# A decoder layer's up-projection: three of its weight tiles formed early instead of two, and the input projection's tiles in a new order

## The chip, the cores and the metric

The kernel runs on one core of a Trainium2 chip. The metric is the device time of one execution in microseconds (us). Before the change the median of three runs is 1663.53 us (1659.94 to 1669.49).

The core has five engines with a queue of instructions each: TensorE (PE in the profile; its weight loads are PEld), VectorE (DVE), ScalarE (ACT), GpSimd (POOL) and SyncE (SP). An engine executes its queue in order, and an instruction that waits holds up those behind it. DMA transfers are issued from the queues of SP, ACT and POOL.

## The reference

One decoder layer for 1024 prompt tokens and 64 sample tokens (8 sequences of 8), 1088 in all, width 1024, in float32:

```python
h = rms_norm(x, norm1) * (1 + scale1) + shift1
z = h @ w_in            # queries, 6 key/value tiles, gates, conv, pooling
x = x + gate1 * (concat[attention, conv, pooling] @ w_out)
h = rms_norm(x, norm2) * (1 + scale2) + shift2
x = x + gate2 * ((silu(h @ w_a) * (h @ w_b)) @ w_down)     # hidden width 2816
```

The queries `q` and two of the key tiles (`ks` for selected blocks, `kw` for the window) are normalised per head after the projection. The raw keys and values `kc`, `vc` are compressed into block keys; this is also done for the sample sequences' paged cache. The pooling mixer takes trailing means over 2, 4, 8 and 16 positions of its two tiles `p0`, `p1`.

## The kernel before, in words

**Precision.** A float32 product is made of three products of "hi" and "lo" parts: ACT copies a tile into a reduced format (hi, line 175), and DVE subtracts hi from it (lo, line 171). Forming a pair of parts is called a split below.

**Stages.** (1) The front: loading x, the adaLN rounds, the first norm, and the values and gates per token. (2) `input_projection` (line 885): 16 weight tiles of 128 columns, each multiplied with the 1088 tokens in three chunks (384, 384, 320). Each tile's weights are loaded into one of two `w_raw` buffers, and split, one tile ahead. In the order of line 901 they are kc, vc, six conv tiles, p0, ks, p1, kw, q0 to q3. (3) Attention for prompt and samples. (4) The output projection and second norm. (5) The up-projection. (6) The down-projection.

**Who sets the order.** The program is emitted by Python generators that share a clock of estimated engine times (`self.t`). `run` (line 85) always continues the ready task with the lowest priority number; `hold` makes a task wait, on that clock, for a condition. So the order of each engine's queue is fixed when the program is built. The tile framework then moves instructions within it by a simulation of its own, and adds the waits that the data and the reuse of buffers need. `late_ada` (16 steps of gate weights) and the compression of three sample sequences run as such tasks beside the input projection. `head_norm` (line 752) is the normalisation of a q, ks or kw chunk: a square on ACT, a matmul with a matrix of means, a square root on ACT, and on DVE a reciprocal (line 765) and a multiplication (line 766). `pooling_steps` (line 815) puts a chain of DVE additions after the last chunk of p0 or p1, then a matmul with the pooling weights, whose result `py` (one buffer) ACT stores to `mix_d`. A `hold` on `pooled` stands after each of the two.

**The up-projection.** Its weights are 22 tiles `j`, each with 128 columns of both halves. Tokens are taken in four quarters of 272, two quarters making a pair `p`. For one tile and one pair the 2 by 2 block product is done with seven products in place of eight (`PRODUCTS`, line 33); each needs a combination of weight blocks, split into hi and lo, and the same for the token blocks. `up` (line 1668) makes one such pass: 7 products of 12 matmuls. `operands` (line 1613) forms the token side of a pair, four times seven combinations (`b_t`) and splits (`b_hi`, `b_lo`). The passes go (0,0), (1,0), (2,0), (2,1), (1,1), (0,1), and from tile 3 on both pairs of one tile; the second pair's operands are formed while the first pair's passes run. `unit_weights` (line 1645) prepares the weights of the next run of passes: for a tile below `AHEAD_W` it loads the 14 ready parts from DRAM (`w_d`, line 1654), for the others it combines (`w_s`) and splits (`w_hi`, `w_lo`) them from two loads of 512 KB (`w_raw`, line 1498):

```python
raw[n] = j if j < AHEAD_W else tuple(self.weight_load(wp, self.i["wup"][j, x]) for x in range(2))
```

**Formed ahead.** `up_weights_ahead` (line 967) forms the seven pairs of one tile and stores them to `w_d`: two loads (`p_raw`), five combinations on POOL, seven splits on ACT and DVE (`p_hl`, two buffers), seven stores of 512 KB on SP's queue. It is called for tile 0 from `first_ahead` (line 961), when the front is done, and for tile 1 beside the four query tiles, in a pool "pre" which takes memory that the pooling tiles had. `self.formed` counts the tiles done. After vc the projection holds until tile 0 is formed, and frees its pool for the conv tiles; after q3 it holds until tile 1 is.

After the projection, attention begins with `key_stacks` (line 1042): the splits `kh`, `kl` of ks, kw and the compressed keys, then the queries' `qh`, `ql`.

Of the kernel before, what the change touches and what calls it, by code (L numbers as in the profile page):

```python
# [32 lines left out]
STORED = {1: 0, 2: 1, 3: 2, 5: 3, 6: 4, 7: 5, 4: 6}  # L33
HID = 2816
NH = HID // P
AHEAD_W = 2
PAGES = 32
NPOOL = 320
NCMP = 255
# [23 lines left out]
class Kernel:  # L63
# [110 lines left out]
    def split(self, hi, lo, src, n, ready=0.0, eng="dve"):  # L174
        self.nc.scalar.activation(hi, src, AF.Copy)  # L175
        r = self.use("act", 0.09 + n * 0.00084, ready)
        return self.combine(lo, src, hi.bitcast(F32), OP.subtract, n, r, eng)
# [707 lines left out]
    def input_projection(self, h):  # L885
        nc = self.nc
        yield from self.hold(lambda: self.ada_loaded >= 8)
        zp_ = self.pool("zout", "left")
        zp = zp_.__enter__()
        self.vt = zp.tile([P, 9, 256], F32, name="vt_")  # L890
        self.gates = zp.tile([P, 9, 24], F32, name="gates")
        self.vcp = zp.tile([64, P], F32, name="vcp")
        self.spawn(0.6, self.first_ahead())
        with self.pool("tok", "left") as tp:
            yield from self.token_part(tp, h)
        yield from self.hold(lambda: self.ahead)
        hn_, hn, pp_ = self.ahead
        zq_ = self.pool("zq", "left")
        self.q = zq_.__enter__().tile([P, 4, T], F32, name="q")
        self.zout = (zq_, zp_)  # L900
        order = ["kc", "vc", "cg0", "ch0", "bg0", "cg1", "ch1", "bg1", "p0", "ks", "p1", "kw", "q0", "q1", "q2", "q3"]
        self.ada2 = self.pool("ada2", "left")
        self.ada_pool = self.ada2.__enter__()
        with self.pool("z", "left") as z:
            load, split, get = self.weights(z, [self.i["win"][ORDER.index(n)] for n in order], raw_bufs=2, bufs=2)

            def tiles(names, step):
                for nm in names:
                    w = get()
                    load()  # L910
                    for ch, (c0, n) in enumerate(CHUNKS):
                        yield max(w[2], max(self.h_at[ch]))
                        acc = self.project(w, h, ch, n)
                        step(nm, ch, acc, c0, n)
                        self.z_steps += 1
                        if ch == 0:
                            split()

            def kcv(nm, ch, acc, c0, n):
                self.evac(self.kcv[:, nm == "vc", c0:c0 + n], acc, n)  # L920

            def qk(nm, ch, acc, c0, n):
                if nm[0] == "q":
                    out, gain, done = self.q[:, int(nm[1]), c0:c0 + n], self.qgain[:, 0:1], None
                else:
                    j = int(nm == "kw")
                    out, gain = self.ksw[:, j, c0:c0 + n], self.kgain[:, 1 + j:2 + j]
                    done = lambda: nc.gpsimd.dma_start(self.o["kskwT"][:, j, c0:c0 + n], out)
                self.spawn(0, self.head_norm(hn, out, acc, n, gain, done=done))

            load()
            load()
            split()
            self.spawn(0.5, self.late_ada())
            yield from tiles(["kc", "vc"], kcv)
            yield from self.hold(lambda: self.formed == 1)
            pp_.__exit__(None, None, None)
            nc.gpsimd.dma_start(self.o["kcvcT"], self.kcv)
            z0 = self.z_steps
            self.spawn(lambda: 0.9 if self.octets <= PACE * (self.z_steps - z0) else 1.5, self.compress_more())  # L940
            with self.pool("conv") as cv:
                for j in range(2):
                    st = dict(zip(("cg", "ch", "bg"), self.conv_steps(cv, j)))
                    yield from tiles([n + str(j) for n in ("cg", "ch", "bg")],
                                     lambda nm, ch, acc, c0, n: st[nm[:2]](ch, acc))
            with self.pool("pooling") as pl:
                self.pooled = 0
                for j, names in ((0, ["ks"]), (1, ["kw"])):
                    step = self.pooling_steps(pl, j)
                    yield from tiles(["p" + str(j)], lambda nm, ch, acc, c0, n: step(ch, acc))  # L950
                    yield from tiles(names, qk)
                    yield from self.hold(lambda: self.pooled > j)
            with self.pool("pre") as pp:
                self.spawn(0.6, self.up_weights_ahead(pp, 1))
                yield from tiles(["q0", "q1", "q2", "q3"], qk)
                yield from self.hold(lambda: self.formed == 2)
            yield from self.hold(lambda: self.prompt_at and self.heads == 18 and 5 in self.ada_at)
            hn_.__exit__(None, None, None)
        self.ada2.__exit__(None, None, None)

    def first_ahead(self):
        yield from self.hold(lambda: self.front_done)
        hn_, pp_ = self.pool("hn"), self.pool("pre")
        self.ahead = hn_, hn_.__enter__(), pp_
        yield from self.up_weights_ahead(pp_.__enter__(), 0)

    def up_weights_ahead(self, pool, j):

# [794 lines left out]
    def ffn(self, wp, fp, H, state, ahead):  # L1763
# [10 lines left out]
        def load(n):  # L1774
            if n < len(runs):
                j = runs[n][0]
                raw[n] = j if j < AHEAD_W else tuple(self.weight_load(wp, self.i["wup"][j, x]) for x in range(2))

# [365 lines left out]
    def build(self):  # L2144
# [32 lines left out]
        self.mix_d = self.dram.tile([P, 8, T], F32, name="mix_d")  # L2177
        self.w_d = self.dram.tile([AHEAD_W, P, 7, 2, 512], F32, name="w_d")
        self.formed = 0
# [155 lines left out]
```

## Time and profile before

| | |
|---|---|
| median of three runs | 1663.53 us |
| the profiled execution's own time | 1667.26 us |
| its span, first to last instruction | 1665.7 us |
| busy: PE, DVE, ACT, POOL | 1567.0, 1091.3, 778.7, 653.4 us |
| mean granted TensorE clock | 0.972 |
| forming of tile 0, first load to last store | 57.5 to 104 us |
| forming of tile 1, first load to last store | 311.6 to 344.5 us |
| first and last load of formed parts in the up-projection | 910.8 and 998.5 us |

In the profile's views, a row of a group names line, engine, operation, output and inputs, their shapes and how often it ran; behind the bar stand the group's busy time, the mean duration of one in ns, and the engine's idle time just before them with what ended it. A row of a view by stretches gives each engine's busy time (and number of instructions), the granted TensorE clock as a share of full speed, and the load of the DMA engines. A row of waits says which instruction waited for which, for how long in all, how often, and the longest. Rows of a timeline start with the time of the start and the duration in us.

### The profile page before, as it was taken

To read this page: it belongs to the slowest core of one execution; us is meant where nothing else is said; L and a number is where in the kernel's file an instruction comes from. 1 tells how busy PE (TensorE), PEld (TensorE's weight loads), DVE (VectorE), ACT (ScalarE), POOL (GpSimd) and SP (SyncE) were. 2 spreads that over 40 slices of the span, in tenths; PEclk is the share of its full clock that TensorE was granted. 3 is DMA by queue.
4 is the path that set the end of the run, shared out by engine and by line. 5 is a ranking of instruction groups with operands and counts; after the bars stand their busy time and mean duration, and the time that the engine had idled before them with its cause. 6 is when DMAs were issued, how large, how long until landed. Compare 5 with 4: busy or idle time off the path is not lost.

```text
span 1665.7 us, 35433 instructions
## 1 busy us (share of the span) xinstructions
PE 1567.0 (94%) x12569; PEld 1393.3 (84%) x12569; DVE 1091.3 (66%) x2646; ACT 778.7 (47%) x1828; POOL 653.4 (39%) x783
## 2 busy tenths in 40 slices
PE   6999999998999899899599989999999999899998
PEld 2899997886777566566399989999999999899998
DVE  4813224876465666766479878776777776477767
ACT  3522215335665567566466534443433443344444
POOL 3111010123343233222013266544555555688765
PEclk9999999997999899999799989999999999999999
DMA  9586664424567363244686554446433435976643
GB/s 334 186 281 179 184 202 155 149 77 149 159 179 220 99 197 101 64 132 134 199 307 196 199 201 173 145 145 212 151 139 139 143 139 197 380 258 245 218 162 125
DMA packets 195923, 302.12 MB, mean 181 GB/s; under 512 B 26353, under 2 KB 133170, under 8 KB 195426
## 3 DMA queue, kind: packets, MB, share of 16 engines
q1 hardware_dynamic: 175874, 272.20, 49.3%
q0 software_dynamic: 5856, 16.24, 3.1%
q10 hardware_dynamic: 14016, 11.41, 2.1%
q8 instruction: 100, 1.64, 0.4%
q14 instruction: 77, 0.63, 0.1%
HBM read 233.43 MB, written 70.53 MB: 182 GB/s over the span
## 4 chain that ended last, share of the span: by engine, by line
PE 75%; DVE 10%; ACT 6%; DMA 4%; issue 3%; POOL 1%; SPq 0%; ACTq 0%; DVEq 0%; POOLq 0%
PE bank L139 72%; PE bank L143 3%; DVE P L1123 2%; ACT P L1135 2%; DVE w_lo L171 1%; DMA w_raw<-in_wup 1%; DMA mixc<-mix_d 1%; DMA x<-x_d 1%; POOL P L1145 1%; DVE b_lo L171 1%; DMA stream<-in_cacheA 1%; ACT w_hi L175 1%; DMA w_raw<-in_wout 1%; DVE x L1889 0%; ACT L1135 0%
## 5 line engine op out<-in xcount | busy, mean ns | idle before, releaser
L139 PE MATMUL bank<-b_hi,w_hi 128*128 128x272 f32 x1232 | 352.3, 291 | 5.9 <-DVE f_g L1686 2.9
L139 PE MATMUL bank<-b_lo,w_hi 128*128 128x272 f32 x1232 | 355.3, 290 | 2.5 <-DVE b_lo L171 2.4
L139 PE MATMUL bank<-b_hi,w_lo 128*128 128x272 f32 x1232 | 350.3, 290 | 0.9 <-DVE w_lo L171 0.9
L139 PEld LDWEIGHTS bank<-b_hi,w_hi 128*128 128x128 f32 x1232 | 231.8, 190 | 9.0 <-ACT b_hi L175 3.8
L139 PEld LDWEIGHTS bank<-b_lo,w_hi 128*128 128x128 f32 x1232 | 234.1, 190 | 3.4 <-DVE b_lo L171 3.3
L139 PEld LDWEIGHTS bank<-b_hi,w_lo 128*128 128x128 f32 x1232 | 232.2, 190 | 1.1 <-DVE w_lo L171 1.1
L1145 POOL TENSOR_SCALAR P<-P,st 128x128 f32<-128x128 f32 (+10 forms) x192 | 109.0, 581 | 232.5 <-DVE st L1141 138.5
L171 DVE TENSOR_TENSOR w_lo<-w_raw,w_hi 128x512 fp32r<-128x512 f32 (+2 forms) x121 | 114.9, 959 | 79.7 <-ACT w_hi L175 79.2
L171 POOL TENSOR_TENSOR w_s<-w_raw 128x512 f32<-128x512 f32 (+1 forms) x88 | 125.2, 1422 | 70.6 <-DVE w_lo L171 52.7
L139 PEld LDWEIGHTS bank<-stream 128*128 128x128 f32 x1056 | 128.4, 200 | 15.7 <-issue 11.9
L175 ACT ACTIVATE w_hi<-w_raw 128x512 fp32r<-128x512 f32 (+2 forms) x122 | 81.1, 679 | 124.0 <-PE bank L139 83.8
L139 PE MATMUL bank<-stream 128*128 128x128 f32 x1056 | 134.6, 286 | 1.7 <-DMA stream<-in_cacheA 1.6
L1135 ACT ACTIVATE P<-P,st 128x128 f32<-128x128 f32 (+12 forms) x192 | 113.1, 590 | 46.1 <-DVE st L1129 29.4
L171 POOL TENSOR_TENSOR x<-x,d_m 128x272 f32<-128x272 f32 x136 | 117.0, 882 | 32.8 <-DVE x L1889 17.4
L139 PE MATMUL bank<-h_hi,w_hi 128*128 128x384 f32 (+1 forms) x384 | 129.3, 337 | 0.4 <-DVE q L766 0.4
L171 DVE TENSOR_TENSOR w_lo<-w_s,w_hi 128x512 fp32r<-128x512 f32 (+1 forms) x124 | 116.4, 940 | 17.2 <-ACT w_hi L175 14.9
L139 PE MATMUL bank<-h_hi,w_lo 128*128 128x384 f32 (+1 forms) x384 | 126.5, 329 | 0.0
L139 PE MATMUL bank<-g,w_hi 128*128 128x272 f32 x616 | 121.1, 292 | 5.7 <-DVE x L1889 5.7
L139 PE MATMUL bank<-h_lo,w_hi 128*128 128x384 f32 (+1 forms) x384 | 126.3, 329 | 0.0
L139 PE MATMUL bank<-g,d_hi 128*128 128x272 f32 x616 | 119.1, 289 | 1.4 <-DVE x L1892 1.2
L1889 DVE SCALAR_TENSOR_TENSOR x<-bank,mod,x 128x272 f32<-128x272 f32 (+1 forms) x200 | 90.1, 476 | 38.9 <-PE bank L139 25.5
L1716 POOL TENSOR_TENSOR f_g<-f_g,f_v 128x272 f32<-128x272 f32 x44 | 43.9, 998 | 152.9 <-DVE f_v L1686 131.7
(373 smaller groups left out, 3789.8 us busy)
## 6 DMA issues: line engine op xcount, KB each, us to landing
g<-g_d SPq DMA_DIRECT2D x63, 544.0 KB, 6.0
g_d<-f_s SPq DMA_DIRECT2D x57, 544.0 KB, 3.4
wada<-in_wada SPq DMA_DIRECT2D x96, 256.0 KB, 5.3
stream<-in_cacheA SPq DMA_DIRECT2D x192, 128.0 KB, 3.2
w_raw<-in_wup SPq DMA_DIRECT2D x40, 512.0 KB, 4.4
unit<-in_cacheB SPq DMA_DIRECT2D x152, 128.0 KB, 2.4
stream<-in_cacheB SPq DMA_DIRECT2D x104, 128.0 KB, 2.4
w_raw<-in_wout SPq DMA_DIRECT2D x24, 512.0 KB, 4.4
```

Of the source, the lines that this page charges most:

```text
L139: return self.nc.tensor.matmul(out, lhsT, rhs, start=start, stop=stop, skip_group_check=chain)
L143: return self.nc.tensor.transpose(out, in_, self.ident if ident is None else ident)
L171: (self.nc.vector if eng == "dve" else self.nc.gpsimd).tensor_tensor(out, a, b, op=op)
L175: self.nc.scalar.activation(hi, src, AF.Copy)
L1123: nc.vector.tensor_tensor_reduce(out=Pt[:, 2 * g + hl, col:col + n], in0=S[g][:, p0:p0 + n], in1=mk, scale=-1.0, scalar=3e38, op0=OP.add, ...
L1135: nc.scalar.activation(Ps, Ps, AF.Exp, scale=-1.0, bias=sy[:, g, 0:1], accum_out=sy[:, g, 1:2])
L1145: nc.gpsimd.tensor_scalar(Ps, Ps, sy[:, g, 3:4], 0.0, op0=OP.mult, op1=OP.add)
L1716: nc.gpsimd.tensor_tensor(g[:, 1], s1, v, op=OP.mult)
L1889: self.last_gate = nc.vector.scalar_tensor_tensor(out[:, :n], acc[:, :n], self.mod[:, 5, m, 0:1], out[:, :n], op0=OP.mult, op1=OP.add)
```

## The change

Tile 2 of the up-projection is formed in the input projection too. `first_ahead` forms tiles 0 and 1, one after the other; tile 2 takes the place of tile 1 beside the last query tiles, of which there are now two there. The order of the input projection becomes kc, vc, ks, kw, the conv tiles, p0, q0, p1, q1, q2, q3. The hold that frees the first "pre" pool stands after kw, and waits for two tiles. In the up-projection the run of tile 2 finds ready parts in `w_d`. `compress_more`, the compression of the prompt's keys, is started after kw in place of after vc.

```diff
-AHEAD_W = 2
+AHEAD_W = 3
...
-        order = ["kc", "vc", "cg0", "ch0", "bg0", "cg1", "ch1", "bg1", "p0", "ks", "p1", "kw", "q0", "q1", "q2", "q3"]
+        order = ["kc", "vc", "ks", "kw", "cg0", "ch0", "bg0", "cg1", "ch1", "bg1", "p0", "q0", "p1", "q1", "q2", "q3"]
...
             yield from tiles(["kc", "vc"], kcv)
-            yield from self.hold(lambda: self.formed == 1)
+            yield from tiles(["ks", "kw"], qk)
+            yield from self.hold(lambda: self.formed == 2)
             pp_.__exit__(None, None, None)
...
-                for j, names in ((0, ["ks"]), (1, ["kw"])):
+                for j, names in ((0, ["q0"]), (1, ["q1"])):
...
             with self.pool("pre") as pp:
-                self.spawn(0.6, self.up_weights_ahead(pp, 1))
-                yield from tiles(["q0", "q1", "q2", "q3"], qk)
-                yield from self.hold(lambda: self.formed == 2)
+                self.spawn(0.6, self.up_weights_ahead(pp, 2))
+                yield from tiles(["q2", "q3"], qk)
+                yield from self.hold(lambda: self.formed == 3)
...
-        yield from self.up_weights_ahead(pp_.__enter__(), 0)
+        pp = pp_.__enter__()
+        for j in range(2):
+            yield from self.up_weights_ahead(pp, j)
```

## The prediction

> **What bounds the kernel now.** I read the page's head first, then its chain of work that ended last, then the stretches of the two places the change touches, and there the waits and groups.
>
> ```profile
> span 1665.7 us, 35433 instructions
> PE 1567.0 (94%) x12569; PEld 1393.3 (84%) x12569; DVE 1091.3 (66%) x2646; ACT 778.7 (47%) x1828; POOL 653.4 (39%) x783
> ...
> PE 75%; DVE 10%; ACT 6%; DMA 4%; issue 3%; POOL 1%; SPq 0%; ACTq 0%; DVEq 0%; POOLq 0%
> ```
>
> TensorE sets the end for three quarters of the span. Time is to be won only where it waits or runs slowly. One such place is the start of the up-projection, where tile 2's weights are formed (columns: stretch, length, busy time and count of PE, PEld, DVE, ACT, POOL, granted clock, DMA):
>
> ```profile
> 946.00:956.00 10.00, 9.95 (x80) 9.73 (x78) 9.77 (x23) 7.54 (x16) 4.16 (x4) 1.00 0.06 20
> 956.00:967.00 11.00, 6.49 (x43) 5.63 (x43) 11.00 (x24) 4.05 (x11) 8.20 (x8) 0.95 0.49 157
> 967.00:973.00 6.00, 5.90 (x27) 5.93 (x28) 5.69 (x9) 2.33 (x6) 5.62 (x8) 0.52 0.30 111
> 973.00:980.00 7.00, 6.99 (x56) 6.77 (x55) 5.76 (x10) 2.57 (x7) 6.24 (x8) 1.00 0.23 82
> 980.00:984.00 4.00, 1.86 (x9) 1.42 (x10) 3.83 (x5) 1.51 (x5) 3.62 (x5) 0.87 0.12 29
> 984.00:990.00 6.00, 6.00 (x28) 5.87 (x28) 2.38 (x6) 1.35 (x4) 1.32 (x2) 0.52 0.98 348
> ```
>
> Undisturbed, PE does 8 matmuls per us (80 in 10 us, the first row). By that rate the next five rows should hold 88, 48, 56, 32 and 48; they hold 43, 27, 56, 9 and 28. What is missing is worth 5.6, 2.6, 0, 2.9 and 2.5 us: 13.6 us lost in 34. Half is waiting, and the rest a granted clock of 0.52 behind each wait. DVE is full in the same rows. The waits of PE from 935 to 1000, and DVE's and POOL's groups from 937 to 986:
>
> ```profile
> PE bank L139 <- DVE f_g L1686: 2.9, 1, 2.9
> PE bank L139 <- DVE b_lo L171: 2.4, 3, 0.8
> PE bank L139 <- DVE w_lo L171: 0.9, 1, 0.9
> PE bank L139 <- ACT b_hi L175: 0.5, 1, 0.5
> ```
> ```profile
> L171 DVE TENSOR_TENSOR b_lo<-b_t,b_hi 128x272 fp32r<-128x272 f32 x19 | 13.9, 761 | 0.2 <-ACT b_hi L175 0.2
> L171 DVE TENSOR_TENSOR w_lo<-w_s,w_hi 128x512 fp32r<-128x512 f32 x5 | 4.0, 794 | 0.0
> L171 DVE TENSOR_TENSOR w_lo<-w_raw,w_hi 128x512 fp32r<-128x512 f32 x2 | 1.4, 686 | 0.2 <-ACT w_hi L175 0.2
> L171 DVE TENSOR_TENSOR w_s<-w_raw 128x512 f32<-128x512 f32 x1 | 0.9, 907 | 0.0
> ...
> L171 POOL TENSOR_TENSOR b_t<-x1b 128x272 f32<-128x272 f32 x20 | 18.9, 961 | 18.3 <-ACT x1b L1603 13.9 <-DVE b_lo L171 2.6 <-issue 1.7
> ```
>
> Every wait of PE there is for DVE, or one step short of it. DVE does three things at once: it forms the second pair's operands (`b_lo`), empties PE's banks (`f_g`), and splits tile 2's weights (`w_lo`, seven in all).
>
> The other place is the end of the input projection:
>
> ```profile
> 104.00:132.00 28.00, 28.00 (x189) 25.82 (x188) 2.41 (x3) 3.60 (x7) 1.66 (x3) 1.00 0.72 228
> 283.00:311.00 28.00, 27.97 (x165) 22.93 (x164) 26.75 (x37) 11.58 (x24) 4.71 (x8) 1.00 0.53 154
> 311.00:339.00 28.00, 27.64 (x161) 26.28 (x160) 20.37 (x29) 10.55 (x21) 7.49 (x7) 1.00 0.45 164
> 339.00:366.00 27.00, 27.00 (x155) 25.68 (x154) 19.67 (x15) 7.30 (x14) 0.00 (x0) 1.00 0.17 59
> 366.00:378.00 12.00, 5.42 (x40) 4.61 (x38) 10.70 (x15) 4.55 (x9) 8.72 (x24) 0.89 0.39 115
> ```
>
> PE is full until 366, while the four query tiles take the third and fourth rows (55 us, 13.7 a tile). Early on DVE is nearly empty (2.41 of 28 us), and full when the pooling runs (26.75). Then comes the step to attention, where PE idles for DVE.
>
> **The change part by part.**
>
> *Tile 2 in the up-projection.* It removes two loads of `w_raw`, five combinations `w_s`, seven `w_hi` on ACT and seven `w_lo`. On DVE that is 4.0 + 1.4 + 0.9 = 6.3 us of the groups above. The work that PE waits for is a queue on DVE without gaps from 946 to 980, so what is taken out of it brings forward everything behind it: the banks emptied, the `x1b` that POOL's `b_t` wait for, and the last `b_lo`. PE gets its last late operand 6.3 us earlier. It doesn't win all 13.6: tile 2's pass then ends about 8 us earlier (5.6 + 2.6), and PE waits in one piece for the second pair's operands, which are late next. I take −6.3. The ends are 0, if POOL or the hand-offs between engines set the operands' pace, and −13.6, if the operands are never late.
>
> It adds 14 loads from `w_d` on SP's queue.
>
> ```profile
> L1654 SPq DMA_DIRECT2D w_hi<-w_d x28: 319/372/639, 910.8 to 998.0; - x28
> L1654 SPq DMA_DIRECT2D w_lo<-w_d x28: 319/383/656, 911.3 to 998.5; - x28
> ...
> DMA to landing us min/median/max: 2.6/4.6/8.7
> ```
>
> A pair of them costs SP some 0.8 us and lands in 4.6 us, 8.7 at worst. The buffers (nine of each) let a part be issued about seven products ahead, that is 84 matmuls or 10.5 us. SP holds only the stores of hidden tiles there, and DMA is at 0.06 in the row from 946. So I take 0, hidden behind the pass before; without that cover it would be 4.6 us once.
>
> *Tiles 0 and 1 in front.* Two loads, five combinations, seven splits and seven stores more run from about 104 to 137 us. DVE and POOL have the room (first row of the last table). On SP the stores wait for each split, and behind them stand the loads of the next weight tile, the gate weights and the cache; PE has a tile in hand. The ks and kw normalisations come to the same place, with their six stores on POOL's queue, behind which stand cache loads. I take 0. The bounds: 0, and +2 if one weight tile comes late once (below: six stores of one forming spread over 15.62 us on SP, less a tile of 13.7).
>
> *Tile 2 beside two query tiles.* Tile 1 was formed beside four:
>
> ```profile
> 320.54 1.29 POOL L171 TENSOR_TENSOR p_hl<-p_raw 128x512 f32<-128x512 f32 x1 [5.49 <-DMA mix_d<-py]
> ...
> 343.51 0.63 DVE L171 TENSOR_TENSOR p_hl<-p_hl 128x512 fp32r<-128x512 f32 x1
> ...
> 324.22 15.62 SPq L985 DMA_DIRECT2D w_d<-p_hl  x6
> ...
> POOL p_hl L171 <- DMA w_d<-p_hl: 12.0, 2, 6.8
> ```
> ```profile
> L765 DVE RECIPROCAL h_sq<-h_sq 128x384 f32<-128x384 f32 x7 | 17.9, 2551 | 13.5 <-ACT h_sq L762 13.5
> L171 DVE TENSOR_TENSOR p_hl<-p_hl 128x512 fp32r<-128x512 f32 x5 | 3.6, 724 | 0.0
> ```
> ```profile
> 366.72 1.05 ACT L175 ACTIVATE kh<-kv__93 128x1024 fp32r<-128x1024 f32 x1
> ...
> 377.83 0.89 PE L139 MATMUL bank<-kh,qh 64*128 64x192 f32 x2 [6.58 <-DVE q L766]
> ```
>
> It can't begin before the pooling's `py` has left the memory, and it took 23.6 us from 320.54 to 344.14, because the two `p_hl` buffers wait for their stores (12.0 us on POOL). The pooling now ends two tiles later, 27.5 us, so the forming ends near 371.6, while the last query product stays at 366. ACT's `kh` at 366.72 and DVE's `kl` then meet the last of the seven splits in their queues. Each split is 0.7 us on DVE and ACT; what must wait is the step to attention, where PE already waits 6.58 us. DVE's room holds the other splits: 19.67 of 27 us are busy from 339 on, without any forming after 344. I take +1.5, two splits; the bounds are 0 (all behind the keys) and +5 (the keys behind all).
>
> *The pooling holds.* After p1 PE has one tile (q1 in place of kw) until the pooling's product, as before. What PE did from 305 to 311.4 beside it:
>
> ```profile
> L139 PE MATMUL bank<-pe_x,pw 128*128 128x384 f32 (+2 forms) x8 | 2.3, 412 | 0.0
> L139 PE MATMUL bank<-wada,sc 128*32 128x512 f32 x8 | 2.1, 604 | 0.0
> ```
>
> The gate steps (`wada`), 2.1 us of fill, may be over by then; PE would idle as long, and do them earlier at no gain. I take 0, since the prompt's compression can fill it; the bounds are 0 and +2.1.
>
> **The sum**: −6.3 + 0 + 0 + 1.5 + 0 = −4.8 us on the profiled execution's 1667.3, which is 1662.5. That execution was 3.7 above the median of the runs, so on the median it is 1663.5 − 4.8 = **1658.7**. Attention's order is planned on clocks that the change shifts; no row prices that.
>
> The Trainium skill (TensorE: Matmul & The Clock Gate, What's actually happening) says that PE falls to half clock after an idle window of some 3.4 us. The trace has 0.52 after a wait of 2.9 us, and again after waits of at most 0.8 us close together, so the trace counts: a single wait of the kind left over by the change still costs a slow stretch. By the rule alone the second stretch, 2.5 us, would not be there before, nor in the 13.6.
>
> **The rivals.**
>
> *All of it is won (0.23).* With the splits gone DVE and POOL finish the second pair in time, as the planner also spreads `b_t` anew. POOL is idle for 13.9 us before its first `b_t`, which speaks for it; that it waits there for DVE's `x1b` speaks against. −13.6 + 1.5: 1651.4.
>
> *Hidden anyway (0.16).* POOL's 20 `b_t` (18.9 us) and their hand-offs pace the operands, and DVE's room goes unused. PE then wins only the wait on `w_lo`, 0.9 us, and gives 1.5 in the tail: about 1664. Against it: POOL itself waits for `b_lo` 2.6 us.
>
> *Slower (0.16): the third forming holds up attention.* With 17.9 us of reciprocals for seven chunks, each 2.55 us long, DVE serves the last three query tiles, the second pooling and the splits. If each of the seven splits waits behind one reciprocal, the forming takes 7 × 2.55 = 17.9 us longer than 23.6, and ends at 389.5. `kh` and `kl` stand behind it on ACT and DVE, so PE starts attention up to 22 us late, and some 16 when the last two splits are passed by. −6.3 + 16.5: 1673.7. It decides from the point where the forming ends more than 6.3 us after `kh` could start, near 373. For it: the forming has half the tiles to hide beside. Against: between reciprocals DVE waited 13.5 us for ACT, which is room.
>
> **How the numbers follow.** My forecast has 0.45, and alone reaches from 1653 to 1664. For 8 in 10 the range takes in most of the first rival and the lower part of the last: 1647 to 1672. A change below 0.5%, 8.3 us, is about what a measurement here can't tell from none, so faster is below 1655.2 and slower above 1671.8. The forecast gives faster 0.18 of its chance and slower 0.03; the first rival 0.8 and 0; the second 0.03 and 0.07; the last 0 and 0.65. In sum faster 0.27, slower 0.13, the same 0.60.
>
> **What would show it.** Right: no split of `w_lo` on DVE between 946 and 966; 35 loads each of `w_hi` and `w_lo` from `w_d` in place of 28; the waits on `f_g` and `w_lo` gone, one wait on `b_lo` or `b_hi` left before pass (2,1); PE full from 104 to 150; the last `p_hl` near 371. Wrong: a row with clock 0.52 as long as before and the same count missing; `kh` later than 373; PE waiting in the query tiles.

## The result

The changed kernel takes 1677.54 us (median of four runs, 1677.41 to 1681.08); beside it the kernel before took 1663.13. The ratio is 1.0081, with a 95% interval of 1.0061 to 1.0101: slower by 14.4 us between the medians and by 10 to 17 us by the interval, where 5 us faster was forecast. The head of the page after, and its chain of work that ended last:

```profile
span 1679.5 us, 35485 instructions
PE 1570.1 (93%) x12569; PEld 1391.5 (83%) x12569; DVE 1091.6 (65%) x2647; ACT 776.7 (46%) x1828; POOL 646.6 (38%) x783
...
PE 61%; DVE 14%; DMA 8%; issue 6%; ACT 6%; POOL 3%; SPq 2%; ACTq 0%; POOLq 0%; DVEq 0%
```

PE's share of the chain fell from 75% to 61%, and DVE's, DMA's and the issue's rose: work that was hidden now sets the end at some places. Where they are is seen when the span is cut at marks that both kernels have. The marks are first and last starts of groups, here of the kernel after (first the product of the input projection, then that of the output projection, the up- and the down-projection):

```profile
L139 PE MATMUL bank<-h_hi,w_lo x384: 302/335/631, 90.6 to 386.6; 128*128 128x384 f32 x128, 128*128 128x320 f32 x64
L139 PE MATMUL bank<-mh,w_hi x256: 283/289/596, 854.4 to 955.2; 128*128 128x272 f32 x128
L139 PE MATMUL bank<-b_hi,w_hi x1232: 282/288/490, 955.6 to 1431.1; 128*128 128x272 f32 x176
L139 PE MATMUL bank<-g,w_hi x616: 283/289/593, 1426.5 to 1663.9; 128*128 128x272 f32 x154
```

and of the kernel before:

```profile
L139 PE MATMUL bank<-h_hi,w_lo x384: 304/335/636, 89.9 to 366.0; 128*128 128x384 f32 x128, 128*128 128x320 f32 x64
L139 PE MATMUL bank<-mh,w_hi x256: 282/289/596, 830.8 to 932.8; 128*128 128x272 f32 x128
L139 PE MATMUL bank<-b_hi,w_hi x1232: 282/288/596, 933.2 to 1417.8; 128*128 128x272 f32 x176
L139 PE MATMUL bank<-g,w_hi x616: 283/289/592, 1413.3 to 1649.8; 128*128 128x272 f32 x154
```

| stage (us) | before | after | difference |
|---|---|---|---|
| front, to the first product of the projection | 89.9 | 90.6 | +0.7 |
| input projection, first to last start of its product | 276.1 | 296.0 | **+19.9** |
| from there to the output projection (mostly attention) | 464.8 | 467.8 | +3.0 |
| output projection and norm | 102.4 | 101.2 | −1.2 |
| up-projection | 480.1 | 470.9 | **−9.2** |
| down-projection to the end of the span | 252.4 | 253.0 | +0.6 |

So the up-projection won more than was forecast, and the input projection lost twice as much as that. The up-projection first: the loads of formed parts, then stretches of its start (columns as in the prediction), then, of PE's waits from 950 to 1430, the two longest at this start (none in the later passes is longer than 1.4 us).

```profile
L1657 SPq DMA_DIRECT2D w_hi<-w_d x35: 319/369/1087, 935.7 to 1009.5; - x35
```
```profile
960.00:970.00 10.00, 10.00 (x81) 9.92 (x80) 9.56 (x21) 8.02 (x17) 0.00 (x0) 1.00 1.01 357
970.00:980.00 10.00, 9.39 (x73) 8.95 (x73) 9.33 (x33) 6.56 (x16) 5.52 (x6) 1.00 0.96 354
980.00:990.00 10.00, 10.00 (x82) 10.00 (x82) 9.50 (x16) 4.61 (x12) 9.62 (x11) 1.00 0.58 188
990.00:1000.00 10.00, 9.52 (x72) 8.82 (x70) 8.87 (x15) 4.23 (x12) 9.04 (x11) 1.00 0.48 145
```
```profile
PE bank L139 <- DMA w_hi<-w_d: 0.5, 1, 0.5
PE bank L139 <- DVE b_lo L171: 0.5, 1, 0.5
```

The clock is 1.00 in every row, and the four rows hold 308 matmuls of the 320 that PE does undisturbed: 1.5 us are missing, where 13.6 were in the 34 us of the prediction. No wait on `f_g` or `w_lo` is left at this place, and DVE splits no `w_lo` there.

Now the input projection: of seven stretches that cover it the three in which PE misses most, and PE's longest waits from 60 to 420:

```profile
120.00:180.00 60.00, 55.38 (x351) 44.81 (x350) 30.51 (x35) 19.16 (x35) 13.55 (x21) 1.00 0.80 265
...
240.00:300.00 60.00, 57.33 (x374) 52.49 (x373) 18.95 (x39) 19.02 (x28) 5.78 (x10) 0.97 0.51 143
...
330.00:360.00 30.00, 24.25 (x134) 21.16 (x133) 22.11 (x33) 8.29 (x16) 1.45 (x2) 0.89 0.04 9
```
```profile
PE bank L139 <- DVE pe_x L869: 4.4, 1, 4.4
PE bank L139 <- ACT vt L622: 3.8, 2, 2.7
PE bank L139 <- DMA stream<-in_cacheA: 3.7, 2, 1.9
PE bank L139 <- DMA wada<-in_wada: 3.4, 2, 2.8
```

Before, PE was full in these stretches; the first of them in the kernel before:

```profile
120.00:180.00 60.00, 60.00 (x410) 55.02 (x408) 17.80 (x37) 11.49 (x21) 7.89 (x14) 1.00 0.67 199
```

Now there are three places. (i) Behind kw, at the hold for two formed tiles, PE waits for gate weights and cache tiles. (ii) Near 285 it waits for ACT's `vt`, a step of the compression. (iii) At 351 to 356, at the end of the tile behind p1, it waits 4.4 us for `pe_x`, the last step of the pooling on DVE, and goes on at about half clock (0.54, last section). Three theories:

- **A, the hold.** The hold for two formed tiles makes the planner put other work in its place.
- **B, the order.** The new order of the tiles itself costs.
- **C, the third forming.** It ends behind the last query tile, and holds up attention (the rival of the prediction).

### The profile page after: what moved, and what is told of

The parts are those of the page before. It is cut to its first block, busy times and chain, and to the rows that moved or that the text cites. A ratio compares the mean times of both kernels' runs of the same rounds, so it can differ in the third digit from the quotient of the medians.

```text
span 1679.5 us, 35485 instructions
## 1 busy us (share of the span) xinstructions
PE 1570.1 (93%) x12569; PEld 1391.5 (83%) x12569; DVE 1091.6 (65%) x2647; ACT 776.7 (46%) x1828; POOL 646.6 (38%) x783
## 4 chain that ended last, share of the span: by engine, by line
PE 61%; DVE 14%; DMA 8%; issue 6%; ACT 6%; POOL 3%; SPq 2%; ACTq 0%; POOLq 0%; DVEq 0%
PE bank L139 57%; PE bank L143 4%; DVE P L1126 2%; DVE w_lo L171 2%; ACT P L1138 2%; SPq L530 1%; DVE b_lo L171 1%; DMA stream<-in_cacheA 1%; DMA w_raw<-in_wup 1%; DMA w_d<-p_hl 1%; DMA w_raw<-in_wout 1%; DVE n_ss L171 1%; DMA x<-x_d 1%; DMA x1b<-in_xT 1%; ACT w_hi L175 1%
## 5 line engine op out<-in xcount | busy, mean ns | idle before, releaser
L171 POOL TENSOR_TENSOR w_s<-w_raw 128x512 f32<-128x512 f32 (+1 forms) x84 | 118.2, 1407 | 58.2 <-DVE w_lo L171 43.2
L171 DVE TENSOR_TENSOR w_lo<-w_s,w_hi 128x512 fp32r<-128x512 f32 (+1 forms) x119 | 112.2, 945 | 16.0 <-ACT w_hi L175 13.6
L1892 DVE SCALAR_TENSOR_TENSOR x<-bank,mod,x 128x272 f32<-128x272 f32 (+1 forms) x200 | 89.9, 475 | 38.2 <-PE bank L139 25.7
```

Of the source, the lines that this page charges most:

```text
L171: (self.nc.vector if eng == "dve" else self.nc.gpsimd).tensor_tensor(out, a, b, op=op)
L1892: self.last_gate = nc.vector.scalar_tensor_tensor(out[:, :n], acc[:, :n], self.mod[:, 5, m, 0:1], out[:, :n], op0=OP.mult, op1=OP.add)
```

## The experiments

The lengths of the input projection and of the stretch from there to the output projection are given as in the table above, from each run's own profile, which is one execution; times are medians, with the ratio to the kernel before in the same series (1666.07, 1666.21 and 1665.80 us in three series). The diffs are shortened: "..." stands for lines and list entries left out.

### The parts of the change one by one

**The new order alone**, with two formed tiles as before:

```diff
# before -> this kernel; AHEAD_W stays 2
-            "kc","vc","cg0",...,"bg1","p0","ks","p1","kw","q0","q1","q2","q3"
+            "kc","vc","ks","kw","cg0",...,"bg1","p0","q0","p1","q1","q2","q3"
+            yield from tiles(["ks", "kw"], qk)
             yield from self.hold(lambda: self.formed == 1)
...
-                for j, names in ((0, ["ks"]), (1, ["kw"])):
+                for j, names in ((0, ["q0"]), (1, ["q1"])):
...
                 self.spawn(0.6, self.up_weights_ahead(pp, 1))
-                yield from tiles(["q0", "q1", "q2", "q3"], qk)
+                yield from tiles(["q2", "q3"], qk)
```

> The new order of the input projection with two tiles formed ahead as before (tile 0 in front, tile 1 beside q2 and q3; the hold after kw waits for one tile). Theory A (the hold for two formed tiles, decided on the planner's clock, is what costs): kw ends long after tile 0 is formed, so nothing is pulled forward; the last query product comes at 366 to 371 us, and with the up-projection as before the time is 1661 to 1669. Theory B (the order itself costs: key normalisations early, queries behind the pooling): the last query product comes at 378 or later and the time is 1674 to 1688.

Measured: 1682.23 us, 1.0106 (1.0086 to 1.0126); the projection takes 287.1 us, 11.0 more than before. B holds, and A is at most a part of the cause. The time is 16.2 us above the kernel before: in the profiles the stretch behind the projection, mostly attention, is 5.1 us longer as well. PE's longest waits up to 375 us are those of the places (ii) and (iii) of the changed kernel:

```profile
PE bank L139 <- DVE pe_x L869: 4.4, 1, 4.4
PE bank L139 <- ACT vt L622: 2.7, 1, 2.7
PE bank L139 <- ACT h_sq L757: 1.3, 1, 1.3
```

**The ready parts alone.** The kernel before, but the passes of tile 2 load the parts of tile 1, which are ready. The up-projection is computed with other weights than tile 2's; the work is that of three formed tiles less one forming.

```diff
-                raw[n] = j if j < AHEAD_W else tuple(self.weight_load(wp, self.i["wup"][j, x]) for x in range(2))
+                raw[n] = min(j, 1) if j < 3 else tuple(self.weight_load(wp, self.i["wup"][j, x]) for x in range(2))
```

> The kernel before, but tile 2's run of passes in the up-projection loads tile 1's ready parts in place of forming its own, so one of 22 hidden tiles is computed with another's weights and no third tile is formed ahead. This prices the up-projection's share alone. If the gain seen with the change (its first matmul to the down-projection's first: 470.9 us in place of 480.1) comes from the forming taken out: 471 us again, time 1652 to 1656. If a different start of the stage made it: 476 or more, time 1659 or more.

Measured: 1653.34 us, 0.9927 (0.9910 to 0.9943). The up-projection takes 468.0 us, 12.1 less than before. That is what the change can win. Up to the up-projection this program is that of the kernel before, so it also shows how far two profiles of the same instructions differ: the projection takes 276.1 us in both, but the stretch from there to the output projection 460.4 us here and 464.8 there.

**The hold without waiting.** The changed kernel, but what is left of tile 1's forming is issued at the hold at once, so that the planner has nothing to wait for:

```diff
-        self.spawn(0.6, self.first_ahead())
+        self.first = self.first_ahead()
+        self.spawn(0.6, self.first)
...
-            yield from self.hold(lambda: self.formed == 2)
+            while self.formed < 2:
+                next(self.first, None)
```

> The changed kernel, but where it held for two formed tiles the rest of the forming is emitted at once, so no other task is emitted in between. Theory A: the stretch from 166 to 194 us, in which PE ran compression and gate steps and waited for their loads, goes; the steps are spread again and fill the later holds; the last query product comes 10 to 18 us earlier than 387 and the time is 1660 to 1669. Theory B: only PE's waits of that stretch, 5 to 6 us, are won; time 1671 to 1674.

Measured: 1675.32 us, 1.0050 (1.0030 to 1.0071); the projection takes 289.9 us, 6.1 less than in the changed kernel. By the ratios the gain is 0.3% or 5 us, with intervals that overlap a little. So A is worth 5 to 6 us, and is not the cause of the rest, as theory B had it (the time is 1.3 us above its range). The same stretch of 28 us, in the changed kernel and in this one:

```profile
165.00:193.00 28.00, 23.34 (x170) 17.17 (x169) 8.63 (x17) 6.74 (x15) 6.45 (x12) 1.00 0.83 265
```
```profile
165.00:193.00 28.00, 28.00 (x186) 25.73 (x185) 9.25 (x14) 5.37 (x11) 4.32 (x8) 1.00 0.57 186
```

In the changed kernel what the hold waits for was done before it began: the last store of tile 1 started at 143.57, while kw's last product ended at 165.65. Yet the next tile's first product starts at 193.74.

```profile
143.57 0.38 SPq L991 DMA_DIRECT2D w_d<-p_hl  x1
...
176.46 1.79 PE L139 MATMUL bank<-wada,sc 128*32 128x512 f32 x4 [2.83 <-DMA wada<-in_wada]
...
184.83 3.59 PE L139 MATMUL bank<-stream 128*128 128x128 f32 x30 [1.83 <-DMA stream<-in_cacheA]
```

So the planner's clock must have put tile 1's end later (this is argued, no view shows that clock), and what it took for a gap was filled with gate steps and compression, whose loads had only just been issued: PE waits there for DMA. That this work is then missing at the later holds, the second half of theory A, is not borne out: without the hold's waiting PE still waits 2.7 us at (ii) and 4.4 at (iii).

**Both late formings beside the queries.** The kernel before with three formed tiles and its old order: tile 0 in front, tiles 1 and 2 one after the other beside q0 to q3.

```diff
-AHEAD_W = 2
+AHEAD_W = 3
...
-                self.spawn(0.6, self.up_weights_ahead(pp, 1))
+                self.spawn(0.6, self.late_ahead(pp))      # tile 1, then tile 2
...
-                yield from self.hold(lambda: self.formed == 2)
+                yield from self.hold(lambda: self.formed == 3)
```

> The order of the kernel before, with tiles 1 and 2 formed one after the other beside the four query tiles, tile 0 in front as before; three tiles ready for the up-projection. Theories A and B: the input projection up to the query tiles as before, the last query product at 366 to 369, the first score matmul up to 5 us late, the up-projection 9 us shorter: 1655 to 1661. Theory C (a forming that ends after the last query tile holds up attention, the slower rival of the prediction): the second forming ends near 372 or later, the first score matmul comes at 385 or later, time 1662 to 1672.

Measured: **1653.16 us, 0.9928 (0.9911 to 0.9944)**. That is below all the ranges, and as much as the ready parts alone win: within the some 3 us of the intervals, a forming beside the queries costs nothing. DVE's last split and ACT's first `kh`, and PE from 330 on:

```profile
366.93 0.63 DVE L171 TENSOR_TENSOR p_hl<-p_hl 128x512 fp32r<-128x512 f32 x1
```
```profile
369.38 1.05 ACT L175 ACTIVATE kh<-kv__93 128x1024 fp32r<-128x1024 f32 x1
```
```profile
330.00:360.00 30.00, 30.00 (x173) 28.59 (x172) 26.79 (x30) 12.98 (x24) 6.61 (x6) 1.00 0.50 186
```

The forming of two tiles ends at 367.6, and attention's first product starts at 373.1, in the kernel before at 377.8 (by the first with `ql` it is 377.6 against 378.5). C expected the forming to end at 372 or later, and so its case doesn't arise here. In the changed kernel it does, the forming ending 4 us behind the last query product; there the step to attention became shorter all the same (see "Why the prediction was wrong"). C falls by that.

**Two tiles in front, old order.** The reverse of the last: tiles 0 and 1 in front with the hold after vc, tile 2 beside four queries.

```diff
-AHEAD_W = 2
+AHEAD_W = 3
...
             yield from tiles(["kc", "vc"], kcv)
-            yield from self.hold(lambda: self.formed == 1)
+            yield from self.hold(lambda: self.formed == 2)
...
-                self.spawn(0.6, self.up_weights_ahead(pp, 1))
+                self.spawn(0.6, self.up_weights_ahead(pp, 2))
...
-        yield from self.up_weights_ahead(pp_.__enter__(), 0)
+        pp = pp_.__enter__()
+        for j in range(2):
+            yield from self.up_weights_ahead(pp, j)
```

> Before's order, but tiles 0 and 1 formed in front with the hold for two formed tiles after the second tile, and tile 2 beside the four queries. If that hold costs about 6 us in any order, as it did in the new one: input projection 281 to 283 us, time 1658 to 1661. If the planner fills it at no cost here: 276 to 277 us, 1652 to 1655. If the order is the whole loss and the hold too is only dear because it comes four tiles in: the second.

Measured: 1669.61 us, 1.0022 (1.0009 to 1.0036), above both expectations; the projection takes 297.9 us, 21.8 more than before. Two stretches, and the largest of PE's waits up to 420:

```profile
104.00:132.00 28.00, 19.08 (x139) 15.79 (x137) 7.25 (x14) 8.75 (x17) 6.56 (x8) 0.91 0.85 296
132.00:160.00 28.00, 20.74 (x150) 18.11 (x151) 8.03 (x15) 6.41 (x14) 7.38 (x11) 0.91 0.96 307
```
```profile
PE bank L139 <- ACT vt L622: 11.1, 2, 8.3
```

Behind vc, two tiles in, the hold falls in the middle of tile 1's forming, and PE loses 16 us in 56. The projection's products pause from 113.3 to 171.1 us, though the last store of tile 1 starts at 141.87: here too the hold lasts some 29 us longer than what it waits for. In the new order the pause is 28 us, and the hold costs 6.1: the keys third and fourth buy something, at a price of their own.

### Why the order costs

Two theories: by F the work that fills PE's waits is over when the pooling comes, by Q the queries are the wrong kind of tile to stand behind it.

**Keys and queries exchanged.** Before's kernel with the pooling at its old place, but q0 and q1 behind the pooling tiles, and ks, kw after them:

```diff
-            ...,"p0","ks","p1","kw","q0","q1","q2","q3"
+            ...,"p0","q0","p1","q1","ks","kw","q2","q3"
...
-                for j, names in ((0, ["ks"]), (1, ["kw"])):
+                for j, names in ((0, ["q0"]), (1, ["q1"])):
...
-                yield from tiles(["q0", "q1", "q2", "q3"], qk)
+                yield from tiles(["ks", "kw", "q2", "q3"], qk)
```

> Before's order and its two formed tiles, but with the first two query tiles behind the pooling tiles and the two key tiles after them, so the pooling stands at its old place and only the kind of tile behind it differs. Theory F expects the input projection within 2 us of before's 276.1 and the time within 4 us of before's 1664 to 1666. Theory Q expects the pooling's waits of the new order here too: 283 to 288 us, time 1673 to 1680.

Measured: 1662.95 us, 0.9985 (0.9969 to 1.0001); the projection takes 277.5 us. What kind of tile follows the pooling doesn't matter: Q falls as a theory of the kind of tile. (Keys are normalised per head as queries are, so this doesn't yet say where the normalisation stands in DVE's queue.)

**The fill paced over 36 steps.** The new order alone, with the compression spread to the pooling's new place:

```diff
-        early = lambda: 0.9 if self.octets * 30 < EARLY * 4 * self.z_steps else 2
+        early = lambda: 0.9 if self.octets * 36 < EARLY * 4 * self.z_steps else 2
```

> Theory F (fill): the new order alone costs because the pooling comes two tiles later, while the filling work (the compression of three sequences, twelve octets) is paced to end after 30 of the tiles' column steps, which was the place of the first pooling hold; here it is paced over 36, the hold's new place. F expects the input projection to fall from 287.1 us to 277 to 282 and the time from 1682 to 1672 to 1677. Theory Q (kind of tile): a query tile behind the pooling puts its head norms on VectorE and ScalarE in front of the pooling's last pieces; Q expects no change, 286 to 288 us and 1680 to 1684.

Measured: 1680.24 us, 1.0096 (1.0062 to 1.0129); the projection takes 288.1 us. The wait at (ii) is gone, and that at (iii) is 6.8 us in place of 4.4. With the same edit the changed kernel without the hold's waiting gives 1671.09 us, 1.0029 (1.0014 to 1.0045), and 290.7 us for the projection: the time falls by 4 us, with intervals that overlap, but the projection, where F had the gain, is 0.8 us longer. What was expected of it:

> The changed kernel with both of the supposed losses taken away: tile 1's forming is issued at once at the hold for two formed tiles, and the compression is paced over 36 steps. Theory F expects an input projection of 279 to 284 us (the changed kernel 296.0, without the hold alone 289.9) and a time of 1665 to 1669. Theory Q expects what the run without the hold showed: 290 us and 1673 to 1677.

The pace isn't the cause: F as I had put it falls too. The trace of the paced order shows why the wait grew, though the profile names no releaser for it: on DVE 6.1 us of other work, with two reciprocals of head norms in it, now stand between the pooling's long step and its last copy, which starts at 346.26; PE's product starts at 346.53.

**The pooling late, the keys not early.** The keys between the convolution and the pooling:

```diff
-            "kc","vc","cg0",...,"bg1","p0","ks","p1","kw","q0","q1","q2","q3"
+            "kc","vc","cg0",...,"bg1","ks","kw","p0","q0","p1","q1","q2","q3"
...
+            yield from tiles(["ks", "kw"], qk)
...
-                for j, names in ((0, ["ks"]), (1, ["kw"])):
+                for j, names in ((0, ["q0"]), (1, ["q1"])):
...
-                yield from tiles(["q0", "q1", "q2", "q3"], qk)
+                yield from tiles(["q2", "q3"], qk)
```

> Before's kernel with the key tiles between the convolution and the pooling, and the queries behind the pooling tiles: the pooling stands as late as in the changed kernel, but the keys don't come third and fourth. Theory P (the pooling's place): the projection takes the 285 to 288 us of the new order, time 1676 to 1682. Theory K (the keys' place in front of the convolution): 276 to 279 us, time 1663 to 1668.

Measured: 1681.06 us, 1.0093 (1.0066 to 1.0121); the projection takes 285.2 us. P holds: 9.1 of the 11.0 us are there with the keys behind the convolution. It is the pooling's place, two tiles later, that costs the most of it. What PE has at the second pooling tile, in the kernel before and in the new order alone (in brackets the wait before, and for what):

```profile
307.27 1.05 PE L139 MATMUL bank<-wada,sc 128*32 128x512 f32 x4
...
309.18 2.24 PE L139 MATMUL bank<-pe_x,pw 128*128 128x384 f32 x7
```
```profile
307.25 1.05 PE L139 MATMUL bank<-wada,sc 128*32 128x512 f32 x4
...
339.78 0.81 PE L139 MATMUL bank<-h_sq,mean_h 128*128 128x320 f32 x2 [1.33 <-ACT h_sq L757]
345.00 3.55 PE L139 MATMUL bank<-pe_x,pw 128*128 128x384 f32 x8 [4.42 <-DVE pe_x L869]
```

The last gate step runs at 307 in both (at 308 to 315 in the other kernels, but for 322 with two tiles in front and the old order). Before, that is inside the second pooling hold; in the new order the pooling's product comes 36 us later, and beside it PE has nothing but one product of a head norm. The chain too ends later, counted from the last product of the tile behind p1: before, that product ends at 305.24 and the chain's last copy at 308.18, 2.9 us later; in the new order at 338.44 and 344.95, 6.5 us later.

**A shorter chain.** DVE in the new order alone, ahead of that product:

```profile
338.78 1.41 DVE L868 SCALAR_TENSOR_TENSOR pe_x<-pe_s,pe_x 64x1208 f32<-64x1208 f32 x1
340.22 0.55 DVE L663 RECIPROCAL ksq<-ksq 128x64 f32<-128x64 f32 x1
...
341.13 2.54 DVE L765 RECIPROCAL h_sq<-h_sq 128x384 f32<-128x384 f32 x1
343.59 1.16 DVE L171 TENSOR_TENSOR w_lo<-w_raw,w_hi 128x1024 fp32r<-128x1024 f32 x1
344.78 0.17 DVE L869 COPY pe_x<-pe_f 64x16 f32<-64x16 f32 x1
```

PE waits for a copy of 0.17 us, and 4.6 us of other work stands in front of it. So the copy is taken away: the first sixteen columns are written in their place, and the long operation leaves them out.

```diff
-                nc.vector.tensor_tensor(f[r_], f[r_], e[r_, 15:31], op=OP.subtract)
-                nc.vector.scalar_tensor_tensor(e[r_, 15:], sg[r_, 15:], iw, e[r_, 15:], ...)
-                nc.vector.tensor_copy(e[r_, 15:31], f[r_])
+                nc.vector.tensor_tensor(e[r_, 15:31], f[r_], e[r_, 15:31], op=OP.subtract)
+                nc.vector.scalar_tensor_tensor(e[r_, 31:], sg[r_, 31:], iw, e[r_, 31:], ...)
```

> The new order alone, two formed tiles, with the pooling's last step on VectorE rewritten so that no copy stands behind the long operation: the sixteen first columns are written in their place and the long operation leaves them out. Theory D (VectorE's order): in the new order the pooling's last copy is queued behind two reciprocals of the first query tiles' head norms (2.5 us each) and a split, and TensorE waits 4.4 us for it and then runs at half clock; D expects the projection to fall from 287.1 us to 280 to 283 and the time from 1680 to 1682 to 1674 to 1677. Theory F2 (nothing left to fill): the tile behind the pooling ends before the chain of the pooling can, whatever stands in it; the projection falls by 2 us at most, and the time stays at 1678 to 1682.

Measured: 1674.26 us, 1.0056 (1.0037 to 1.0075); the projection takes 281.9 us, 5.2 less, and PE's stretch is whole again but for a wait of 1.3 us:

```profile
330.00:360.00 30.00, 28.67 (x167) 26.20 (x166) 24.16 (x29) 10.98 (x21) 1.28 (x1) 1.00 0.25 81
```
```profile
342.43 2.06 PE L139 MATMUL bank<-pe_x,pw 128*128 128x384 f32 x8
```

D holds: the wait for `pe_x` is gone. The product that took 3.55 us at the lower clock takes 2.06. Of the two head norms' reciprocals that D names, one stood ahead of the long step (at 336.17) and one behind it. One is left in front of the chain's end even now, for in DVE's queue the short subtraction was put behind the long step and a reciprocal:

```profile
338.99 2.55 DVE L765 RECIPROCAL h_sq<-h_sq 128x384 f32<-128x384 f32 x1
341.58 0.17 DVE L867 TENSOR_TENSOR pe_x<-pe_f,pe_x 64x16 f32<-64x16 f32 x1
```

It ends 1.3 us behind the tile's last product (340.45), where the copy ended 6.5 behind it. What is left of the order's 11.0 us are 5.8, of which 4.6 are waits for `vt` (2.7), `h_sq` (1.3) and `ada_s` (0.6). No run takes these away, and why a later pooling puts other work in front of the chain's end in DVE's queue is not shown.

**The changed kernel mended twice**, without the hold's waiting and with the shorter chain:

> The changed kernel without the planner's wait at the hold for two formed tiles and with the pooling's last copy taken out of the chain. D expects the projection at 283 to 286 us (without the hold alone 289.9) and a time of 1668 to 1672; F2 expects 288 to 290 us and 1673 to 1677.

Measured: 1668.06 us, 1.0013 (0.9994 to 1.0031); the projection takes 283.3 us. Both losses add: 6.1 and 6.6 us. Mended so far, the change is where it began: the gain in the up-projection (468.6 us) only pays for the 7.2 us by which the projection is still longer and the 2.2 us in the stretch behind it.

**The best order with keys and queries exchanged**: tiles 1 and 2 late, and the exchange of above.

> Tile 0 in front as before, tiles 1 and 2 formed beside the last four tiles, and the queries behind the pooling tiles with the keys after them. The forming of tiles 1 and 2 late gave 0.9928 of before's time and the exchange of keys and queries 0.9985; if both hold together, 0.989 to 0.993, 1648 to 1655 us. If the attention waits for the keys' parts as they now come later, 1655 to 1660 us.

Measured: 1655.63 us, 0.9937 (0.9917 to 0.9957): the exchange adds nothing. The time lies at the edge between the two expectations. The stretch behind the projection is 464.2 us, 3.5 longer than with the old order, which is no more than two profiles of the same instructions differ by; so it isn't shown that attention waits for the keys. The best kernel is the one with both late formings in the old order, faster than the kernel before by 0.56 to 0.89% and so than the changed kernel.

## Why the prediction was wrong

The step that failed is **"The pooling holds"**, taken as 0 with bounds of 0 and +2.1. Measured with the new order alone it is +11.0 us. The bounds rested on one row, the 2.1 us of gate steps that filled the second hold, and on the belief that the prompt's compression can fill it. That the gate steps may be over by then was named, and they were: the last one ran at 307 us with the pooling at either place. Wrong was the price of that. The compression didn't fill the hold, and the chain's end was taken to come as soon after the tile as before. It came 3.6 us later, since other work stands in front of its last instruction in DVE's queue: PE waited 1.3 us for a head norm and 4.4 for the copy, and the lower clock came behind. Taking the wait for the copy away gave back 5.2 of the 11.0 us. The other 5.8 are for the most part waits, with `vt` above all at a place that the prediction did not look at; why the new order brings them stays open.

**"Tiles 0 and 1 in front"**, 0 with +2 at most: the forming itself added 2.8 us (289.9 less 287.1, the projection without the hold's waiting against the order alone; a small difference of two single profiles), and the hold 6.1. I asked if the engines had room, and they nearly had (PE busy 44.2 of the 46 us from 104 to 150); the larger cost came from the hold for two tiles, which the sum has no term for. The parts of the projection, 11.0 + 2.8 + 6.1 = 19.9 us, add up by construction. The medians, which are independent of that, agree: the order alone is 1.06% dearer, the ready parts 0.73% cheaper and the hold's waiting 0.31% dearer, in sum 0.64% of the 0.81% measured, which leaves 0.17%, or 2.8 us, for the third forming itself.

**"Tile 2 in the up-projection"**, −6.3 with ends of 0 and −13.6: the mechanism was right, the size was off. The ready parts alone won 12.1 us, the changed kernel 9.2. That is the first rival's case: the operands of the second pair are in time once the splits are gone. The prediction left over 7.3 us (13.6 less 6.3), a wait for them in one piece with a slow stretch; what came is a wait of 0.5 us for `b_lo`, at full clock. The 14 loads, taken as 0, cost one wait of 0.5 us.

**"Tile 2 beside two query tiles"**, +1.5: the step to attention, from the last product of the projection to attention's first, became shorter. It is 11.8 us before (366.0 to 377.8), and 6.4 in the changed kernel, with 386.6 from the table's mark and the first product here:

```profile
389.78 0.62 DVE L171 TENSOR_TENSOR p_hl<-p_hl 128x512 fp32r<-128x512 f32 x1
...
393.04 0.36 PE L139 MATMUL bank<-kh,qh 64*128 64x192 f32 x2 [0.93 <-DVE q L766]
396.15 0.36 PE L139 MATMUL bank<-kl,qh 64*128 64x192 f32 x2 [2.76 <-DVE kl L171]
```

But then PE waits for `kl`, which the prediction had named. By attention's first product with `ql` the two kernels are even (12.5 us before, 11.7 after). The forming ended at 390, as in the last rival (389.5), but for another reason: the whole projection was 20 us late, and the forming with it. `kh` came later than 373 as well (389.0), as that rival would have it, and PE waited in a query tile, at (iii). So two of the signs that were named as wrong did appear, and their cause was not the one tied to them. That the rival's 1673.7 us lies near the 1677.5 measured is luck.

**What stays open.** The stretch from the projection to the output projection is 3.0 us longer in the changed kernel. In the eight profiles with the late pooling it takes 466.2 to 472.1 us, in the six with the pooling at its old place 458.0 to 464.8. So the late pooling seems to cost some us in attention as well, but no run here tells by what, and two profiles of the same instructions differed there by 4.4. Nor do the runs tell why the changed kernel won 9.2 us in the up-projection and not 12; the six kernels that form tile 2 there take 478.8 to 481.7 us for it in their profiles, the eight with three ready tiles 467.8 to 470.9, so a part of that difference may be no more than scatter.

## What to carry to other kernels

Work that fills a wait is there for a stretch of time; whoever moves the wait should look for what still runs at the new place, and for what the last instruction of the chain stands behind on its engine. A hold on a planner's clock can have a price of its own, even where the thing waited for is long done. Try the gain alone first, with the work that pays for it left out: it showed here that 12 us were to be had, and putting the new forming beside work that had room, without moving a tile, got them.

## What the runs showed of the hardware

A reciprocal of 128x384 takes 2.54 us on DVE, the long step of the pooling over 1208 columns 1.41 (rows above): 6.6 and 1.2 ns a column. So one reciprocal in front of a short instruction costs more than the chain's longest step. By the Trainium skill (VectorE: DVE Perf Modes, First, the fixed hardware budget), a reciprocal is an iterative division with a repeat count of 8; the rows agree in direction, with a ratio of 5.7 in the time of a column.

The clock in the changed kernel, behind the waits at the places (i), (ii) and (iii):

```profile
176.00:180.00 4.00, 3.54 (x20) 2.10 (x21) 0.00 (x0) 0.00 (x0) 0.00 (x0) 1.00 0.88 314
...
288.00:292.00 4.00, 4.00 (x16) 4.00 (x15) 1.61 (x5) 0.24 (x1) 0.00 (x0) 0.57 0.45 130
...
356.00:360.00 4.00, 4.00 (x10) 2.61 (x11) 3.13 (x4) 0.58 (x1) 0.00 (x0) 0.54 0.14 49
```

Behind a wait of 2.8 us at (i) it stayed at 1.00, behind one of 2.7 us at (ii) it fell to 0.57, behind 4.4 us at (iii) to 0.54. So with the first two the length of the wait alone doesn't tell if a slow stretch follows.
